# Two-layer hybrid decoder trunk: the opening's first two projections in float32 on h as loaded, with the norm's factor applied afterwards

## The chip, the cores and the metric

The kernel runs on one core of one Trainium2 chip. The metric is the device time of one execution in microseconds (us); the median of three runs is given. Engines are called by their profile names: PE (matrix engine, with PEld its weight loads), DVE (vector), ACT (scalar), POOL (GpSimd) and SP (the queue that issues the loads).

## The reference

A sequence of 528 positions (16 learned meta tokens and 512 real ones) with 1024 features goes through two layers. Everything is float32.

```
def mixer_sublayer(h, pre_g, ...):
    u = rms_norm(h, pre_g)                     # h * rsqrt(mean(h*h) + eps) * pre_g
    z = u @ w_in                               # q, k, v, forget logit, conv value and gate, short conv b, c, x
    y_attn = forgetting_attention(q, k, v, log_sigmoid(f_logit + b_forget))
    a = a_val * sigmoid(a_gate)                # conformer module
    a = silu(layer_norm(causal_depthwise_conv(a, 31 taps) + bias))
    y_conv = a @ a_pw_w
    y_sc = sc_b * causal_depthwise_conv(sc_c * sc_x, 3 taps)
    return h + rms_norm(head_rms_norm(concat[y_attn, y_conv, y_sc]) @ w_out, post_g)

def ffn_sublayer(h, ...):
    z = causal_depthwise_conv(rms_norm(h, pre_g) @ w_up, 3 taps)
    return h + rms_norm((silu(g) * up) @ w_down, post_g)

def reference(x, ...):
    h = concat[meta_tokens, x]
    for l in range(2):
        h = ffn_sublayer(mixer_sublayer(h, ...), ...)
    return h[16:]
```

## The kernel before

Activations lie transposed: features on the 128 partitions in KD = 8 blocks `k`, the 528 positions along the free axis. They are worked in two halves of H = 264 positions; `hf` is 0 or 1. So a projection of 128 output columns for one half is a sum over 8 blocks of 128x128 weights times 128x264 activations.

Weights come in chunks of 512 KB in the order in which they are used. A chunk is loaded into a `raw` tile (a ring of three), ACT rounds it into `whi` (L617) and DVE writes the rest into `wlo` (L621). Activations are split in the same way into `uhi` and `ulo` (ACT L816, DVE L817). `mm3` (L642, the matmul is L648) then makes each product out of three matmuls, hi by hi, hi by lo and lo by hi, so one projection of one half is 24 matmuls of 264 columns.

In the planned parts every engine follows an order written out when the kernel is built. `Flow` (L219) keeps, for each engine and for SP, a list of operations with an estimated duration, a priority (the lowest number goes first) and what they wait for; it plays them against estimated times and writes each out when its turn comes. PE is driven by threads that yield what they wait for. On the chip the order of an engine then stands fixed and only its waits move.

The opening, up to the mixer of layer 0, is planned in L1741 to L1755 and runs as follows.

- `load_h` issues `h`, two blocks at a time, the first half ahead of the second; `plan_w` issues the weight chunks. The per-feature vectors `pv` of both layers are loaded through POOL's queue (L405) and DVE scales the gains into `pg` (L407).
- For each half, `Norms.square` has ACT square `h` (L723) and DVE add the squares up (L732). `Norms.factor` sums over the features with matmuls against the constant `om_d` (L772) and makes the factor of the norm in ACT (L782, L785, L786) and DVE (L787, L793).
- `gained` multiplies `h` by the gain (ACT L802, tile `hg`), and `pre_norm` multiplies by the factor (DVE L814) and splits the result into `uhi` and `ulo`.
- `First` holds the first six projections, numbered 0 to 5: conv gate and value for two blocks of 128 features (0 and 1, 2 and 3), short-conv c (4) and x (5). `first_half` starts them for half 0 as soon as its `uhi` and `ulo` are there. Half 1 of the same six projections is started in `mixer` (`firsts`, L945).
- `gated` (L914) evacuates a gate and a value: exp, ln, exp on ACT (L918 to L920), one product on DVE (L921) into `apad`. When both halves of a block are there, `conv_taps` (L937) puts 31 taps for each block on DVE (L929, L932) at the lowest priority; `conv_tail` (L1488) needs the last of them for its means on PE (L1500).

PSUM has eight banks: two pairs for the ring "mm" (0 and 1, 5 and 6), banks 2 and 3 for "s", banks 4 and 7 for "n".

Of the kernel before, what the change touches and what calls it, by code (L numbers as in the profile page):

```python
# [15 lines left out]
P = 128  # L16
# [33 lines left out]
NP = 6  # L50

# [304 lines left out]
def tile_hybrid_trunk(ctx: ExitStack, tc: tile.TileContext, xT, wflat, pv_d, out):  # L356
# [46 lines left out]
    for l in range(DEPTH):  # L403
        pv = T(const, [P, NPV], F32, f"pv{l}")
        nc.gpsimd.dma_start(pv, pv_d[l])  # L405
        pg = T(const, [P, NGAIN], F32, f"pg{l}")
        nc.vector.tensor_scalar_mul(pg, pv[:, :NGAIN], -0.5)  # L407
        pvs.append((pv, pg))

# [47 lines left out]
    def load_h(pool, src, prio=0):  # L457
# [3 lines left out]
            t[:, k0:k0 + 2, half_sl(hf)], src[:, k0:k0 + 2, half_sl(hf)]), prio=prio + 3 * hf, lat=dma_lat(2 * H))  # L461
# [142 lines left out]
    def plan_block(i, prio):  # L604
# [19 lines left out]
        got = flow.op("sp", dma_us(sz), load, prio=prio, lat=dma_lat(sz), takes=[(raws, slot)])  # L624
        ring = split["pw"][chunks[i][1]] if chunks[i][0] == "a_pw_w" else split["wide" if i in wide else "rot"]
        a = act(act_us(sz), high, got, prio=prio, takes=[(ring, b.slot)])
# [33 lines left out]
    class First:  # L660
# [4 lines left out]
        def __init__(self, rhs, n, at):  # L665
            self.rhs, self.n, self.at = rhs, n, at
            self.ws, self.ps, self.tok = [], {}, {}
            self.slot = {(hf, i): Slot() for hf in range(2) for i in range(max(FIRST.values()))}

# [26 lines left out]
    class Norms:  # L696
# [17 lines left out]
        def square(self, key, k, src, n, *after, prio=1):  # L714
# [14 lines left out]
            else:  # L729
                a = act(us, lambda: squares(lambda: self.c_tile(n)), *after, prio=prio, takes=[(self.c, slot)])  # L730
                if k < KD - 2 * apart:
                    s["at"] = dve(dve_us(2 * n), lambda: nc.vector.tensor_add(s["acc"]["c"], s["acc"]["c"], box["c"]),  # L732
                                  a, s["at"], prio=prio)
# [155 lines left out]
    def mixer(l, ypool, first, close_first, spans):  # L889
# [7 lines left out]

        mp = ms.enter_context(tc.tile_pool(name=f"mp{l}", bufs=1, reuse_waits="tile"))
# [6 lines left out]
        conv, apads, sigs = [], [], []  # L905
        for j in range(2):
            sigs.append(T(mp, [P, L], F32, ("sccx", "cxp")[j]))
            apad = T(mp, [P, L + CK - 1], F32, "apad", 2)
            nc.gpsimd.memset(apad[:, :CK - 1], 0.0)
            apads.append(apad)  # L910
            conv.append(T(mp, [P, L], F32, "cacc", 2))
        gated_at = {}

        def gated(hf, j, tok):  # L914
            c = half_sl(hf)
            sig = sigs[j][:, c]
            us = act_us(H)
            a = a0 = act(us, lambda: nc.scalar.activation(sig, first.ps[hf, 2 * j], AF.Exp, scale=-1.0), tok)  # L918
            b = act(us, lambda: nc.scalar.activation(sig, sig, AF.Ln, bias=c_one), a)
            b = act(us, lambda: nc.scalar.activation(sig, sig, AF.Exp, scale=-1.0), b)  # L920
            gated_at[hf, j] = got = dve(dve_us(H), lambda: nc.vector.tensor_mul(  # L921
                apads[j][:, CK - 1 + H * hf:CK - 1 + H * (hf + 1)], first.ps[hf, 2 * j + 1], sig), b, prio=0)
            for i in range(2):
                first.slot[hf, 2 * j + i].close(a0, got)
# [31 lines left out]
        for j in range(2):  # L956
            gated(0, j, first.tok[0, 2 * j + 1])
# [6 lines left out]
        def sc_c(j):  # L964
            t = sc[j] = T(mp, [P, L], F32, "sccx")

            def use(hf, ps, tok):
# [6 lines left out]
        def sc_x(j):  # L974
            t = sc[j]
            cx = T(mp, [P, L + 2], F32, "cxp")
# [10 lines left out]
            def use(hf, ps, tok):  # L987
# [26 lines left out]
        for i, make in ((4, sc_c), (5, sc_x)):  # L1014
            use = make(0)
            for hf in range(2):
                evacs += use(hf, first.ps[hf, i], first.tok[hf, 5])
# [84 lines left out]
        def sc_norm(j):  # L1102
            sq = T(mp, [P, L + 2], F32, "cxp")[:, :L]
# [849 lines left out]
```

## Time and profile before

| | us |
|---|---|
| three runs | 1317.92, 1320.25, 1321.16 |
| median | 1320.25 |
| the profiled execution | 1320.06 |
| its span on the core | 1318.4 |
| PE busy in the span | 1278.1 |
| DVE busy | 859.1 |
| ACT busy | 626.3 |
| POOL busy | 98.9 |

The profile is of one execution. A row of its timeline gives start, duration, engine, line of the kernel, operation, tile written and tiles read, and in brackets how long the engine had been idle before it and what released it. Matmuls overlap in the pipeline, so their pace is the distance between starts and not the duration of one. Instructions of DVE and ACT overlap by a little as well. A float32 matmul shows as two records.

### The profile page before, as it was taken

How to read it: one execution, taken by the hardware profiler on the slowest of the kernel's cores; microseconds unless marked ns; L12 is line 12 of the kernel's file. 1: busy time of each engine (PE TensorE's matmuls, PEld its weight loads, DVE VectorE, ACT ScalarE, POOL GpSimd, SP SyncE). 2: the span in 40 equal slices, each digit the busy share in tenths (PEclk: the TensorE clock that was granted, in tenths of full speed). 3: DMA queues.
4: the chain of work that ended last, by engine and by line, in shares of the span. 5: the costliest groups of instructions: out<-in, count | busy, mean ns of one | idle time of the engine just before them, and what ended most of it. 6: DMA issues, size and time to landing. Idle time of an engine off the chain costs nothing. (4 is left out here: it accounts for less than half of the span.)

```text
span 1318.4 us, 23824 instructions
## 1 busy us (share of the span) xinstructions
PE 1278.1 (97%) x9758; PEld 1223.3 (93%) x9758; DVE 859.1 (65%) x1450; ACT 626.3 (48%) x1176; POOL 98.9 (8%) x255
## 2 busy tenths in 40 slices
PE   5999999999999999999989999999999999999997
PEld 4989898999999999999989898979999799989997
DVE  6588856488633674576575888666877247646764
ACT  7345568555423432234662555685644233323353
POOL 1313321000000000000003223110000000000000
PEclk9999999999999999999989999999999999999999
DMA  7032120602222222223240322116032222232221
GB/s 247 21 98 75 56 75 33 213 30 85 92 97 81 97 86 91 96 86 106 82 163 17 99 82 65 57 54 214 24 97 85 92 97 95 71 108 97 90 71 65
DMA packets 42700, 118.26 MB, mean 90 GB/s; under 512 B 4848, under 2 KB 15088, under 8 KB 42592
## 3 DMA queue, kind: packets, MB, share of 16 engines
q1 hardware_dynamic: 42496, 116.48, 26.6%
q8 instruction: 77, 1.26, 0.4%
q0 software_dynamic: 96, 0.26, 0.1%
q14 instruction: 31, 0.25, 0.1%
HBM read 108.04 MB, written 4.33 MB: 85 GB/s over the span
## 5 line engine op out<-in xcount | busy, mean ns | idle before, releaser
L648 PE MATMUL psum<-uhi,whi 128*128 128x264 f32 (+1 forms) x1984 | 466.9, 288 | 7.4 <-ACT uhi L816 7.4
L648 PE MATMUL psum<-ulo,whi 128*128 128x264 f32 (+1 forms) x1984 | 461.7, 285 | 0.9 <-DVE ulo L817 0.9
L648 PE MATMUL psum<-uhi,wlo 128*128 128x264 f32 (+1 forms) x1984 | 459.7, 284 | 0.0
L648 PEld LDWEIGHTS psum<-uhi,whi 128*128 128x128 f32 x1984 | 333.4, 189 | 11.6 <-ACT uhi L816 8.6
L648 PEld LDWEIGHTS psum<-ulo,whi 128*128 128x128 f32 x1984 | 334.2, 190 | 1.9 <-DVE ulo L817 1.5
L648 PEld LDWEIGHTS psum<-uhi,wlo 128*128 128x128 f32 x1984 | 334.0, 190 | 0.0
L648 PE MATMUL psum<-yhi,whi 128*128 128x264 f32 (+3 forms) x840 | 235.2, 304 | 1.4 <-ACT yp L1885 1.0
L648 PE MATMUL psum<-ylo,whi 128*128 128x264 f32 (+3 forms) x840 | 232.6, 300 | 1.0 <-DVE ylo L1085 0.8
L648 PE MATMUL psum<-yhi,wlo 128*128 128x264 f32 (+3 forms) x840 | 231.7, 299 | 0.5 <-DVE wlo L621 0.5
L503 ACT CAST whi<-raw 128x1024 fp32r<-128x1024 f32 (+1 forms) x110 | 113.5, 1033 | 212.5 <-PE psum L648 198.9
L504 DVE TENSOR_TENSOR wlo<-raw,whi 128x1024 fp32r<-128x1024 f32 (+1 forms) x110 | 132.0, 1201 | 81.5 <-ACT whi L503 79.5
L648 PEld LDWEIGHTS psum<-yhi,whi 128*128 128x128 f32 x840 | 150.0, 188 | 10.2 <-ACT yp L1885 1.4
L648 PEld LDWEIGHTS psum<-ylo,whi 128*128 128x128 f32 x840 | 150.0, 188 | 7.5 <-DVE ylo L1085 2.0
L648 PEld LDWEIGHTS psum<-yhi,wlo 128*128 128x128 f32 x840 | 150.2, 188 | 6.1 <-DVE wlo L621 0.9
L1834 DVE SCALAR_TENSOR_TENSOR c<-z,pv,c 128x528 f32<-128x528 f32 (+1 forms) x176 | 132.2, 757 | 2.7
L621 DVE TENSOR_TENSOR wlo<-raw,whi 128x1024 fp32r<-128x1024 f32 (+2 forms) x86 | 102.5, 1207 | 43.0 <-ACT whi L617 42.5
L617 ACT CAST whi<-raw 128x1024 fp32r<-128x1024 f32 (+2 forms) x86 | 87.9, 1035 | 35.8 <-DMA raw<-in_w_dram 17.4
L932 DVE SCALAR_TENSOR_TENSOR cacc<-apad,pv,cacc 128x528 f32<-128x528 f32 x120 | 87.6, 773 | 0.5
L1852 ACT CAST yhi<-c 128x528 fp32r<-128x528 f32 (+1 forms) x44 | 27.6, 628 | 111.3 <-DVE c L1848 111.3
L1844 ACT ACTIVATE c<-c 128x528 f32<-128x528 f32 (+1 forms) x44 | 28.2, 640 | 81.7 <-DVE c L1834 81.7
L1832 ACT ACTIVATE c<-z,pv 128x528 f32<-128x528 f32 (+1 forms) x88 | 63.5, 728 | 0.0
L1797 DVE TENSOR_TENSOR z<-psum,rz 128x528 f32<-128x528 f32 x40 | 28.3, 709 | 53.7 <-PE psum L648 52.1
(199 smaller groups left out, 1422.1 us busy)
## 6 DMA issues: line engine op xcount, KB each, us to landing
raw<-in_w_dram SPq DMA_DIRECT2D x160, 512.0 KB
raw<-in_w_dram SPq DMA_DIRECT2D x32, 448.0 KB
h<-in_x_dram SPq DMA_DIRECT2D x16, 264.0 KB
raw<-in_w_dram SPq DMA_DIRECT2D x4, 528.0 KB
q<-q SPq DMA_DIRECT2D x16, 132.0 KB
k<-k SPq DMA_DIRECT2D x16, 132.0 KB
h_dram<-h SPq DMA_DIRECT2D x4, 528.0 KB
h<-h_dram SPq DMA_DIRECT2D x8, 264.0 KB
```

What stands on the lines that cost most here:

```text
L503: nc.scalar.copy(hi[:, :sz], raw[:, :sz])
L504: nc.vector.tensor_sub(lo[:, :sz], raw[:, :sz], hi[:, :sz].bitcast(F32))
L617: nc.scalar.copy(box["hi"][:, :sz], box["raw"][:, :sz])
L621: nc.vector.tensor_sub(lo[:, :sz], box["raw"][:, :sz], box["hi"][:, :sz].bitcast(F32))
L648: nc.tensor.matmul(d, lhsT=w[a][:, k, cols], rhs=rhs(b, k, hf), start=start and i == 0 and p == 0, stop=stop and i == n - 1 and p == 2)
L932: nc.vector.scalar_tensor_tensor(conv[j], in0=src, in1=conv[j], scalar=col("a_dw_w", CK * j + i), op0=ALU.mult, op1=ALU.add)
L1797: nc.vector.tensor_mul(two(t[:, off:]), srcs[0], two(rz))
L1832: nc.scalar.activation(dst, src[:, 2:2 + 2 * fw], AF.Copy, scale=wtap(2, t))
L1834: nc.vector.scalar_tensor_tensor(dst, in0=src[:, i:i + 2 * fw], scalar=wtap(i, t), in1=dst, op0=ALU.mult, op1=ALU.add)
L1844: silu = nc.scalar.activation(cs[0], cs[0], AF.Silu)
L1852: nc.scalar.copy(ghi, cs[0])
```

## The change

- **Two projections on h as loaded.** Projections 0 and 1 of half 0 become 8 float32 matmuls each on `h` itself. Their weights are multiplied by the gain first, projection 0 by DVE, projection 1 by POOL, each in two pieces of 128x512, into tiles that the mixer uses later (`apad`, `cacc`).
- **The factor of the norm afterwards.** Projections 2 to 5 of half 0 use the split of `h` times the gain (`u_raw`: ACT for hi, DVE for lo, held in `ypool`), without the factor. The factor of half 0 (`rz0`) is applied when the six products leave PSUM: in `gated` by two more DVE products, in `sc_c` by two DVE products in place of an ACT copy. Half 0 of `uhi` and `ulo`, which later projections read, is still made, by `normed`, with priority after half 1.
- **Half 1** is as before, but the gain and the factor are applied by one DVE instruction for each block in place of ACT L802 and DVE L814.
- **Sums of squares** of both halves are added by POOL in place of DVE (six additions of 128x528).
- **Loads.** The gains of layer 0 come first on SP, then `h` and the halves of chunks 0 and 1 in turn, chunks 2 and 3, then half 1 of `h` in turn with chunks 4 and 5. Chunks 0 and 1 have tiles of their own beside the ring of three. The rest of the vectors follows on SP, behind these; POOL issues no load.
- **Warm-up.** 24 matmuls of 264 columns on a tile of ones go ahead of everything on PE.
- `ypool` and the tiles of the conv and short conv (`Front`, pool `mq`) are opened ahead of the opening's pool.

```diff
-        nc.gpsimd.dma_start(pv, pv_d[l])
...
-        nc.vector.tensor_scalar_mul(pg, pv[:, :NGAIN], -0.5)
+    nc.sync.dma_start(pvs[0][0][:, :NGAIN], pv_d[0][:, :NGAIN])
+    nc.vector.tensor_scalar_mul(pvs[0][1], pvs[0][0][:, :NGAIN], -0.5)
...
+        def alone(self, hf, both, *ids, whole=None):
+            slots = [(yield from flow.grab(pring[0]["mm" if both else "s"], self.slot[hf, ids[0]]))]
+            t = mmt(slots[0].buf) if both else psum[:, slots[0].buf]
+            for j, i in enumerate(ids):
+                self.ps[hf, i] = t[:, j, :self.n[hf]] if both else t[:, :self.n[hf]]
+                if i < 2:
+                    for k in range(KD):
+                        yield whole[i](k)
+                        nc.tensor.matmul(self.ps[hf, i], lhsT=whole[2][i][k // 4][:, k % 4], rhs=whole[3](k), start=k == 0, stop=k == KD - 1)
+                        self.tok[hf, i] = flow.mm(mm4_us(self.n[hf]))
+                        yield
+                    continue
+                yield [self.ws[i].tok]
+                for k in range(KD):
+                    yield [When(lambda: self.at.get((hf, k)))]
+                    mm3({hf: self.ps[hf, i]}, self.ws[i].w, [k], self.rhs, start=k == 0, stop=k == KD - 1)
...
+                        s["at"] = gp(add, lambda: nc.gpsimd.tensor_add(s["acc"]["c"], s["acc"]["c"], box["c"]),
+                                     a, s["at"], prio=prio)
...
+        def gated(self, hf, j, tok, rz=None, rz_at=None):
...
+            if rz is not None:
+                a = b = dve(dve_us(H), lambda: nc.vector.tensor_mul(sig, gate, rz), tok, rz_at, prio=0)
...
+            if rz is not None:
+                b = dve(dve_us(H), lambda: nc.vector.tensor_mul(sig, sig, rz), b, prio=0)
...
+                if rz is not None:
+                    e = dve(dve_us(H), lambda: nc.vector.tensor_mul(t[:, c], ps, rz), tok, prio=0)
+                    sc_at[j, "c", hf] = dve(dve_us(H), lambda: nc.vector.tensor_mul(t[:, c], t[:, c], rz), e, prio=0)
+                    return [e]
...
+        warm = T(sp, [P, H], F32R, "warm", 1)
+        nc.vector.memset(warm.bitcast(F32), 1.0)
+        for i in range(WARM):
+            nc.tensor.matmul(psum[:, 7, :H], lhsT=warm[:, :P], rhs=warm, start=True, stop=True)
...
+        def with_gain(i, j, raw, got):
+            c = slice(4 * j, 4 * j + 4)
+            eng, on, us = ((nc.vector, dve, dve_us(4 * P)), (nc.gpsimd, gp, 1.2))[i]
+            wg_at[i].append(on(us, lambda: eng.tensor_mul(
+                wg[i][j], raw()[:, 4 * P * j:4 * P * (j + 1)].rearrange("p (k n) -> p k n", n=P),
+                g0[:, c].unsqueeze(2).to_broadcast([P, 4, P])), got, prio=-1))
...
+        plan_block(0, 0.6, loads=[(0.01, 1.5), (0.03, 1.5)], also=lambda *a: with_gain(0, *a))
+        plan_block(1, 0.6, loads=[(0.1, 1.5), (0.11, 1.5)], also=lambda *a: with_gain(1, *a))
+        h, h_at = load_h(sp, xT, apart=0.27, step=0.01, late=1.5)
+        [plan_block(i, 0.2 + 0.02 * i) for i in range(wpos[0], FIRST["ffn_w_down"])]; wpos[0] = FIRST["ffn_w_down"]
+        flow.op("sp", 0.4, lambda: nc.sync.dma_start(pvs[0][0][:, NGAIN:], pv_d[0][:, NGAIN:]), prio=3.5)
+        pv1 = flow.op("sp", 0.4, lambda: nc.sync.dma_start(pvs[1][0], pv_d[1]), prio=3.5, lat=2.0)
...
+        for k in range(KD):
+            hk, hi, lo, gc = h[:, k, :H], u_raw[0][k], u_raw[1][k], g0[:, k:k + 1]
+            c = act(act_us(H) + 0.06, lambda hk=hk, hi=hi, gc=gc: nc.scalar.activation(hi, hk, AF.Copy, scale=gc),
+                    h_at[0, k - k % 2], prio=0)
+            d = dve(stt_us(H), lambda hk=hk, hi=hi, lo=lo, gc=gc: nc.vector.scalar_tensor_tensor(
+                lo, in0=hk, scalar=gc, in1=hi.bitcast(F32), op0=ALU.mult, op1=ALU.subtract), c, prio=0)
...
+                reads.setdefault((hf, k), []).append(
+                    norms.square(("h", hf), k, h[:, k:k + 2, half_sl(hf)], H, h_at[hf, k], prio=0.3 - 0.08 * hf, add=1.2))
...
+        def normed(hf, prio):
...
+            yield from norms.factor(key, H, out=None if hf else rz0)
...
+                f = [dve(stt_us(H), lambda k=k, i=i: nc.vector.scalar_tensor_tensor(
+                    h[:, k + i, c], in0=h[:, k + i, c], scalar=g0[:, k + i:k + i + 1], in1=s["r"],
+                    op0=ALU.mult, op1=ALU.mult), *f, prio=prio + 0.01 * k) for i in range(2)]
+                hi = act(act_us(2 * H), lambda k=k: nc.scalar.copy(uhi[:, k:k + 2, c], h[:, k:k + 2, c]), *f,
+                         prio=prio + 0.01 * k)
+                lo = dve(dve_us(2 * H), lambda k=k: nc.vector.tensor_sub(
+                    ulo[:, k:k + 2, c], h[:, k:k + 2, c], uhi[:, k:k + 2, c].bitcast(F32)), hi, prio=prio + 0.01 * k)
...
+        def opening():
+            for j in range(2):
+                yield from first.alone(0, True, 2 * j, 2 * j + 1, whole=(
+                    lambda k: [wg_at[0][k // 4], h_at[0, k - k % 2]], lambda k: [wg_at[1][k // 4], h_at[0, k - k % 2]],
+                    wg, lambda k: h[:, k, :H]))
+                front.gated(0, j, first.tok[0, 2 * j + 1], rz0, rz_at)
+            for i in (4, 5):
+                yield from first.alone(0, False, i)
...
+        flow.thread(normed(0, 1.2))
+        flow.thread(normed(1, 0.7))
+        flow.thread(opening())
```

More of the change, by code (lines that the diff above doesn't have):

```diff
@@ L50 @@
 NP = 6
+WARM, WARM_US = 24, 4.5
 _COLS = {}
@@ L902, in mixer @@
         zero = Tok(0.0)
[L905 to L924, printed above, removed]
+        conv, apads, gated_at, gated = front.conv, front.apads, front.at, front.gated
         def tap(j, i):
@@ L954, in firsts @@
             yield from first.steps(1, (True, 4, 5))
-        for j in range(2):
-            gated(0, j, first.tok[0, 2 * j + 1])
+        if not begun_front:
+            for j in range(2):
+                gated(0, j, first.tok[0, 2 * j + 1])
         flow.thread(firsts())
@@ new lines, in tile_hybrid_trunk @@
+        rz_at = When(lambda: [norms.sums["h", 0]["r_at"]] if "r_at" in norms.sums["h", 0] else None)
+        def opening():
+            for j in range(2):
+                yield from first.alone(0, True, 2 * j, 2 * j + 1, whole=(
[4 more added lines that the diff above has]
+                yield from first.alone(0, False, i)
```

123 lines of the change are left out of this document (94 added, 29 removed).

## The prediction

> **What bounds the kernel now.** I read the page first, then the busy time by stretches, then PE's waits up to 130 us, then the timeline of the opening, engine by engine. The page and the three stretches (busy us, records in brackets, granted clock, DMA share, GB/s):
>
> ```profile
> span 1318.4 us, 23824 instructions
> PE 1278.1 (97%) x9758; PEld 1223.3 (93%) x9758; DVE 859.1 (65%) x1450; ACT 626.3 (48%) x1176; POOL 98.9 (8%) x255
> 0.00:17.00 17.00, 2.10 (x4) 1.17 (x4) 8.22 (x13) 12.73 (x22) 4.30 (x25) 1.00 0.88 301
> 17.00:38.00 21.00, 20.33 (x144) 19.90 (x145) 17.49 (x24) 14.79 (x26) 0.19 (x2) 1.00 0.44 149
> 38.00:1318.40 1280.40, 1255.66 (x9612) 1202.27 (x9610) 833.35 (x1415) 598.73 (x1129) 94.42 (x228) 1.00 0.26 86
> ```
>
> PE is the bound: idle for 1318.4 - 1278.1 = 40.3 us, 14.9 of them in the first 17 us and 24.7 spread over the last 1280. Only the first part can be attacked by this change. PE's waits there (total, times, longest) and its timeline:
>
> ```profile
> PE psum L772 <- DVE acc L732: 8.7, 1, 8.7
> PE psum L648 <- ACT uhi L816: 6.3, 1, 6.3
> 8.66 2.10 PE L772 MATMUL psum<-acc,om_d 128*128 128x264 f32 x4 [8.66 <-DVE acc L732]
> 17.07 0.59 PE L648 MATMUL psum<-uhi,whi 128*128 128x264 f32 x1 [6.31 <-ACT uhi L816]
> 18.26 0.59 PE L648 MATMUL psum<-ulo,whi 128*128 128x264 f32 x1 [0.60 <-DVE ulo L817]
> 19.31 0.42 PE L648 MATMUL psum<-uhi,wlo 128*128 128x264 f32 x1
> 19.53 0.42 PE L648 MATMUL psum<-uhi,whi 128*128 128x264 f32 x1
> ...
> 22.37 0.28 PE L648 MATMUL psum<-ulo,whi 128*128 128x264 f32 x1
> 22.48 0.28 PE L648 MATMUL psum<-uhi,wlo 128*128 128x264 f32 x1
> ...
> 25.05 0.28 PE L648 MATMUL psum<-uhi,wlo 128*128 128x264 f32 x1
> 25.16 0.29 PE L648 MATMUL psum<-uhi,whi 128*128 128x264 f32 x1
> 28.86 1.05 PE L772 MATMUL psum<-acc,om_d 128*128 128x264 f32 x4
> 29.55 0.48 PE L648 MATMUL psum<-uhi,whi 128*128 128x264 f32 x1
> 29.87 0.28 PE L648 MATMUL psum<-ulo,whi 128*128 128x264 f32 x1
> ```
>
> PE waits for the sum of squares until 8.66 and for the normalised first half until 17.07. It then runs at 0.22 us between starts until about 22.2 and at 0.12 us after that: about 18 matmuls cost 0.1 us more each, 1.8 us. The granted clock is 1.00 in all stretches and does not show this step; the pace does. [...]
>
> Half 0 of the six projections is 6 x 24 = 144 split matmuls. The second stretch holds 144 records, 4 of them L772, so 4 are left at 38.0 and half 1 starts at 38.0 + 4 x 0.12 = 38.4. From there on PE runs on nearly without a break, so the time hangs on S, the start of half 1: profiled time = 1320.06 - (38.4 - S) + whatever the rest loses. The 1320.06 of the profiled execution is 1.66 above its span and within 0.2 of the median 1320.25.
>
> **PE's own sum after the change.** A float32 matmul of 264 columns, from L772 at 28.86 to the regular place of the next matmul: L648 at 29.87 less one step is 29.75, so 0.89 us for two, 0.445 each. Projections 0 and 1: 16 x 0.445 = 7.1. Projections 2 to 5: 96 x 0.1215 (pace at 25 us) = 11.7. Two norm sums: 2 x 0.89 = 1.8. Together 20.6 us. Against three split matmuls (0.365) float32 costs 16 x 0.08 = 1.3 us more; the norm sum of half 0 (0.9) moves from idle time into the stream.
>
> **When PE can begin.** Loads, the engines that follow them, and DVE's group of additions up to 38.2 us (busy us, mean ns of one, idle before):
>
> ```profile
> 0.81 1.97 SPq L460 DMA_DIRECT2D h<-in_x_dram  x4
> 3.55 0.65 ACT L723 ACTIVATE acc<-h 128x528 f32<-128x528 f32 x1 [1.46 <-DMA h<-in_x_dram]
> 6.32 1.33 ACT L723 ACTIVATE c<-h 128x528 f32<-128x528 f32 x2 [0.34 <-DMA h<-in_x_dram]
> GB/s 0 0 0 27 205 287 342 411 333 368 256 382 395 381 393 369 410 418 418 411 353 387 387 378 365 369 227 434 336 98 147 328 328 279 246 270 221 164 16 0
> L732 DVE TENSOR_TENSOR acc<-acc,c 128x528 f32<-128x528 f32 x6 | 4.2, 707 | 1.6 <-ACT c L723 1.3
> ```
>
> The first 0.26 MB of `h` are there at 3.5, the third at 6.3, and the queue moves some 0.39 MB per us (the GB/s row, half-us slices up to 20 us). With the small gains load ahead (+0.5 us): first `h` about 4, first half of chunk 0 near 5, last of the first half of `h` near 8, chunk 1 in halves at 8.5 and 9.2, chunk 2 at 10.5, chunk 3 at 12, chunk 4 at 14, last of half 1 at 16. DVE needs 0.7 us for a piece of gained weights (128x512; L732 takes 0.71 for 528 columns), so projection 0 can start near 6. The warm-up covers that: 24 matmuls x 0.22 = 5.3 us from about 1 us. It costs nothing while it ends before the first gained weights; if its tile of ones is written late, behind the gains on DVE, projection 0 starts 2 us later, which the wait for projection 1's weights half absorbs. Its gain is the 1.8 us of slow pace.
>
> So S is at least 6.2 + 20.6 = 26.8, that is 11.6 us earlier than now.
>
> **What ACT, DVE and POOL must do by then.** Mean ns per instruction, from the other groups up to 38.2 us, L866's group of the whole span and two single rows:
>
> ```profile
> L621 DVE TENSOR_TENSOR wlo<-raw,whi 128x1024 fp32r<-128x1024 f32 (+1 forms) x8 | 9.8, 1231 | 3.6 <-ACT whi L617 3.6
> L817 DVE TENSOR_TENSOR ulo<-hg,uhi 128x528 fp32r<-128x528 f32 x8 | 5.4, 703 | 0.7 <-ACT uhi L816 0.7
> L793 DVE SCALAR_TENSOR_TENSOR rs<-rs 128x264 f32<-128x264 f32 x2 | 0.9, 434 | 0.1
> L617 ACT CAST whi<-raw 128x1024 fp32r<-128x1024 f32 (+1 forms) x8 | 8.4, 1047 | 0.6 <-DMA raw<-in_w_dram 0.6
> L802 ACT ACTIVATE hg<-h,pg 128x264 f32<-128x264 f32 x16 | 6.9, 506 | 0.7 <-DVE pg L407 0.7
> L816 ACT CAST uhi<-hg 128x528 fp32r<-128x528 f32 x8 | 5.0, 635 | 3.8 <-DVE hg L814 3.8
> L723 ACT ACTIVATE c<-h 128x528 f32<-128x528 f32 x6 | 3.7, 638 | 0.4 <-DMA h<-in_x_dram 0.3
> L866 DVE SCALAR_TENSOR_TENSOR ulo<-h,pg,uhi 128x264 fp32r<-128x264 f32 x24 | 11.0, 491 | 0.0
> 33.06 1.87 ACT L816 CAST uhi<-hg 128x528 fp32r<-128x528 f32 x3 [1.71 <-DVE hg L814]
> 40.01 0.43 DVE L921 TENSOR_TENSOR apad<-psum,sccx 128x264 f32<-128x264 f32 x1 [1.86 <-ACT sccx L920]
> ```
>
> ACT up to the first pair of half 1: 8 hi parts x 0.51, 8 squares x 0.64, 6 chunks x 1.05, two norms of three passes and two gates of three passes at 0.43 (as DVE's passes of 264 columns), one pair 0.64: 4.1 + 5.1 + 6.3 + 2.6 + 2.6 + 0.6 = 21.3 us from 4, which ends at 25.3. The removed products by the gain (16 x 0.51) are half replaced by the hi parts. ACT just fits.
>
> DVE: gained weights 2 x 0.7, lo parts 8 x 0.49, six chunks 7.4, two norms 4 x 0.43, two gates 6 x 0.43 (four more than now, 1.7 us), first pair 2 x 0.49 + 0.70: 1.4 + 3.9 + 7.4 + 1.7 + 2.6 + 1.7 = 18.7 us from 5, which ends at 23.7. The half-0 normalisation (8 x 0.49 + 4 x 0.70 = 6.7) is put behind half 1 and lies beside half 1's 17.5 us on PE. The six additions (4.2) are gone from DVE. In `sc_c` one ACT copy becomes two DVE products, 0.9 us, with DVE idle around it. The loads of the remaining vectors wait behind all of these on SP and are wanted only by the taps.
>
> POOL's rows:
>
> ```profile
> L1391 POOL TENSOR_SCALAR_AFFINE_SELECT pf<-pf x64: 289/295/1492, 94.7 to 874.0; 128x128 f32<-128x128 f32 x64
> L1348 POOL TENSOR_SCALAR dm<-ident,mcol x80: 270/374/1286, 86.7 to 846.2; 128x128 fp32r<-128x128 f32 x64, 16x16 fp32r<-16x16 f32 x16
> 89.90 1.22 DVE L621 TENSOR_TENSOR wlo<-raw,whi 128x1024 fp32r<-128x1024 f32 x1
> 90.08 1.28 POOL L1348 TENSOR_SCALAR dm<-ident,mcol 128x128 fp32r<-128x128 f32 x1 [0.99 <-DVE mcol L1340]
> ```
>
> POOL takes six additions and two gained pieces (the groups give min, median and max ns). No POOL row has two tensor inputs, so I bound it: below by DVE's 0.71, above by twice 528/128 of POOL's undisturbed 0.295 for 128 columns and one input (median of L1391), 2.4. I take one pass in proportion, 1.2 us; eight are 9.6 us.
>
> [...]
>
> These rows also speak against the change: POOL's row at 90.08 lies beside a DVE instruction with two inputs from SBUF, and it took 1.28 instead of 0.37 (median), until just after DVE ended at 91.12. So additions on POOL do not simply leave DVE. Suppose POOL and those DVE instructions never overlap: 18.7 less the eight of 0.43 that read PSUM (3.4) is 15.3, plus 9.6 is 24.9 from 5, so the first pair of half 1 is there at 29.9. Without any exclusion it is PE's 26.8. DVE has gaps (it waits for ACT's chunks), so part of POOL's time falls into them. I take S = 29.0, nearer to the excluded end, as DVE is busy 18.7 of 24 us. The later pairs of half 1 cost DVE 1.7 us each against 1.46 for PE (12 x 0.1215), three pairs: 0.7 us more. **Forecast: 1320.06 - (38.4 - 29.0) + 0.7 = 1311.4 us.**
>
> **Rivals.**
>
> *The POOL chain ends last.* PE's order is fixed, and the norm sum of half 0 stands ahead of the later projections. Its chain is additions on POOL, with the gained weights of projection 1 in the same queue: five instructions from about 7.6 us, 13.6 undisturbed. If each is held by one chunk on DVE (1.28 - 0.37 = 0.9), it is 18, and the same again in half 1 puts its factor 4 us later than in the forecast: S = 33.0, time 1314.7 + 0.7 = 1315.4. For it: the row at 90.08. Against: DVE's short instructions early on. [...]
>
> *PE's own work is the only limit.* S = 26.8 and no loss after: 1308.5. For it: ACT and DVE fit by their sums. Against: 25.3 on ACT leaves 1.5 us for every hop and late load.
>
> *The second half is not earlier.* Its `uhi` is made from 33.06 on now, after ACT and DVE work that the change keeps and adds to (hi and lo parts, gates). If all the delays add up, the first pair comes at 36.5: 1320.06 - 1.9 = 1318.2, within 0.3%.
>
> *Slower: DVE's backlog reaches the conv tail.* The last tap and its reader on PE:
>
> ```profile
> 169.58 0.76 DVE L932 SCALAR_TENSOR_TENSOR cacc<-apad,pv,cacc 128x528 f32<-128x528 f32 x1
> 184.17 0.77 DVE L1504 TENSOR_TENSOR cacc<-cacc,psum 128x264 f32<-128x264 f32 x2 [1.10 <-PE psum L1500]
> ```
>
> Taps run at the lowest priority and end at 170.3, 13.8 us ahead of their reader. PE comes 9 us earlier, which leaves 5. DVE's added work is 3.9 + 1.4 + 1.7 + 0.9, and 16 x 0.49 in place of L814's eight (taken at L817's 0.70: 2.2 more), less 4.2: 5.9 us, plus up to 9.6 held by POOL; DVE's idle time up to 38 us (38.0 - 8.2 - 17.5 = 12.3) takes it. It decides only when the backlog passes 12.3 + 5; each us more is a us of PE if the order has nothing else in that place. To lose the whole gain of 8.7 and 5 us it takes 13.7 more than that: 1325.
>
> **How the numbers follow.** Forecast 0.42, POOL chain 0.25, PE alone 0.15, second half not earlier 0.11, slower 0.07. Faster by over 0.3% (4 us, about what a measurement of this kernel can tell from no change) is the first three, 0.82; within 0.3% 0.11; slower 0.07. The range 1307 to 1317 holds the first three and leaves out the last two; its lower end is PE alone less 1.5 us, since the order of the mixer is planned anew and some of PE's 24.7 us of later idle time lies there.
>
> **What would show it.** Right: projection 0 starts near 6 us at a pace of 0.445; split matmuls run at 0.12 from their first; PE has no wait over 3 us after it; half 1 starts at 28 to 30; POOL's additions take 1.0 to 1.5 us, and longer beside DVE's chunks; the mixer's waits stay. Wrong: L772 or projection 1 waits over 3 us for POOL (first rival); the start of half 1 waits for DVE or ACT until 33 or later (third); L1500 waits for a tap (fourth); or the pace of 0.22 comes back because PE went idle between the warm-up and projection 1.

## The result and the profile after

The changed kernel takes 1316.66 us (median of 16 executions, 1312.88 to 1318.85) against 1320.11 us before (16 executions, 1317.43 to 1323.27): a ratio of 0.9971, 95% interval 0.9961 to 0.9982. The forecast was 1311.4, 8.7 us less than before; 3.5 came. The interval leaves out 1, though 3.5 us is under the 4 that the prediction took for measurable, and the time lies inside the stated range. The profiled execution of the changed kernel was its fastest, 1312.88 us at a mean granted clock of 0.998; the 16 together have 0.9944, and 58 executions of the kernel before, timed beside the runs below, have 0.997. That difference turns out to be a part of the answer.

The page of the kernel after, and the same three stretches as before (busy us with records, clock, DMA share, GB/s):

```profile
span 1311.2 us, 23868 instructions
PE 1281.2 (98%) x9766; PEld 1225.1 (93%) x9766; DVE 869.9 (66%) x1469; ACT 622.2 (47%) x1167; POOL 108.3 (8%) x261
0.00:17.00 17.00, 13.32 (x59) 11.40 (x59) 11.41 (x14) 11.05 (x18) 9.65 (x30) 1.00 0.87 295
17.00:38.00 21.00, 19.83 (x150) 18.96 (x151) 20.79 (x36) 14.59 (x27) 4.78 (x3) 1.00 0.30 105
38.00:1311.20 1273.20, 1248.07 (x9560) 1194.72 (x9558) 837.73 (x1421) 596.54 (x1124) 93.90 (x228) 1.00 0.28 87
```

In the first 17 us PE works 13.3 us (5.4 of them the warm-up) instead of 2.1. DVE is busy 20.8 of the next 21 us, where it was 17.5. PE's waits up to 60 us (total, times, longest):

```profile
PE psum L667 <- DVE wlo L624: 1.9, 1, 1.9
PE psum L667 <- ACT uhi L1870: 0.8, 1, 0.8
PE psum L698 <- POOL cacc L1829: 0.4, 1, 0.4
PE psum L667 <- DVE ulo L1872: 0.4, 1, 0.4
```

and the timeline of the opening after, PE first, then DVE and POOL, then the forget gate of layer 0 (start, duration, idle before):

```profile
1.26 5.37 PE L1819 MATMUL psum<-warm 128*128 128x264 f32 x24 [1.26 <-DVE warm L1817]
6.47 4.08 PE L698 MATMUL psum<-h,apad 128*128 128x264 f32 x16
10.97 3.83 PE L698 MATMUL psum<-h,cacc 128*128 128x264 f32 x16 [0.43 <-POOL cacc L1829]
16.91 0.39 PE L667 MATMUL psum<-yhi,wlo 128*128 128x264 f32 x1 [1.88 <-DVE wlo L624]
17.14 1.05 PE L815 MATMUL psum<-acc,om_d 128*128 128x264 f32 x4
31.45 0.39 PE L667 MATMUL psum<-uhi,whi 128*128 128x264 f32 x1 [0.79 <-ACT uhi L1870]
32.22 0.39 PE L667 MATMUL psum<-ulo,whi 128*128 128x264 f32 x1 [0.38 <-DVE ulo L1872]
...
8.33 7.40 DVE L1848 SCALAR_TENSOR_TENSOR ylo<-h,pg,yhi 128x264 fp32r<-128x264 f32 x6
22.45 1.43 DVE L1866 SCALAR_TENSOR_TENSOR h<-h,pg,rz 128x264 f32<-128x264 f32 x2
8.36 1.31 POOL L775 TENSOR_TENSOR acc<-acc,c 128x528 f32<-128x528 f32 x1 [4.41 <-ACT c L762]
9.88 2.23 POOL L1829 TENSOR_TENSOR cacc<-raw,pg 128x512 f32<-128x512 f32 x2 [0.20 <-DMA raw<-in_w_dram]
...
72.58 0.41 PE L1283 MATMUL psum<-fpre,ones_r 128*128 128x40 f32 x2 [0.71 <-DVE fpre L1278]
74.50 0.60 PE L1292 MATMUL psum<-ident,gt 128*8 128x128 f32 x4 [0.71 <-DVE gt L1284]
```

PE begins at 6.47, as forecast. Half 1 runs without a break from 32.22, where one of its matmuls is done, so S, the effective start of half 1, is 32.1: 6.3 us earlier than 38.4. The span is 7.2 shorter.

### The profile page after: what moved, and what is told of

It reads as the page before. It is cut to its first block, busy times and chain, and to the rows that moved or that the text cites. A ratio compares the mean times of both kernels' runs of the same rounds, so it can differ in the third digit from the quotient of the medians.

```text
span 1311.2 us, 23868 instructions
## 1 busy us (share of the span) xinstructions
PE 1281.2 (98%) x9766; PEld 1225.1 (93%) x9766; DVE 869.9 (66%) x1469; ACT 622.2 (47%) x1167; POOL 108.3 (8%) x261
## 5 line engine op out<-in xcount | busy, mean ns | idle before, releaser
L667 PE MATMUL psum<-uhi,whi 128*128 128x264 f32 (+1 forms) x1936 | 451.4, 287 | 1.9 <-ACT uhi L859 1.1
L667 PE MATMUL psum<-ulo,whi 128*128 128x264 f32 (+1 forms) x1936 | 446.6, 284 | 0.7 <-DVE ulo L1872 0.4
L667 PE MATMUL psum<-uhi,wlo 128*128 128x264 f32 (+1 forms) x1936 | 444.7, 283 | 0.0
L667 PEld LDWEIGHTS psum<-uhi,whi 128*128 128x128 f32 x1936 | 322.7, 189 | 5.5 <-issue 2.4
L667 PEld LDWEIGHTS psum<-ulo,whi 128*128 128x128 f32 x1936 | 323.7, 189 | 1.6 <-DVE ulo L860 0.7
L667 PEld LDWEIGHTS psum<-uhi,wlo 128*128 128x128 f32 x1936 | 323.6, 189 | 0.0
L667 PE MATMUL psum<-yhi,whi 128*128 128x264 f32 (+3 forms) x872 | 245.2, 304 | 1.5 <-ACT yp L2025 1.0
L667 PE MATMUL psum<-yhi,wlo 128*128 128x264 f32 (+3 forms) x872 | 240.9, 299 | 2.4 <-DVE wlo L624 2.4
L667 PE MATMUL psum<-ylo,whi 128*128 128x264 f32 (+3 forms) x872 | 241.2, 299 | 1.0 <-DVE ylo L1152 0.8
L667 PEld LDWEIGHTS psum<-ylo,whi 128*128 128x128 f32 x872 | 156.2, 188 | 7.6 <-DVE ylo L1152 2.0
```

The lines of the kernel that those rows point to most:

```text
L667: nc.tensor.matmul(d, lhsT=w[a][:, k, cols], rhs=rhs(b, k, hf), start=start and i == 0 and p == 0, stop=stop and i == n - 1 and p == 2)
```

## Experiments

The theories named in the expectations are "POOL holds DVE" (six additions and two gained pieces on POOL slow the DVE instructions beside them down, and half 1 is late by that) and "clock" (more of its executions run some stretches at half clock). All runs were timed in five rounds beside the kernel before, unless said otherwise.

**The same kernel again.** No edit.

> The changed kernel once more, to see how its executions differ. In the profiled execution (1312.88 us, granted clock 0.998) half 1 starts at about 32.1 us instead of 38.4, which is worth 6.3 us; the median of 16 executions is only 3.5 us under the one of before, and its granted clock is mostly 0.992 to 0.996. Theory (clock): in most executions the clock falls to half in the opening, in PE's wait of 1.9 us for a chunk's low part at 14.8 us or at the half-1 start at 30.5 us; then the recorded clock steps show a stretch of some 3.4 to 6.8 us at half clock before 40 us, and times rise by about 1 us for each 0.1% of clock. Rival (later loss): the stretches at half clock all lie at the layer boundary near 660 us and at the end, as in the profiled execution, and there is no step in the opening; then the gain that is missing was never there and the profiled execution was only lucky.

1315.01 us (7 executions, mean clock 0.9951), ratio 0.9967 (0.9954 to 0.9981). Again the profiled execution was the fastest (1312.6 at 0.998) and shows no stretch at half clock before 661 us, so it could not show the step that the theory wanted. The 7 executions here and the 16 above differ by 1.65 us in their medians; together with the single one below, all 24 have 1316.66 us.

**The additions back on DVE.**

```
-  norms.square(("h", hf), k, ..., prio=0.3 - 0.08 * hf, add=1.2))
+  norms.square(("h", hf), k, ..., prio=0.3 - 0.08 * hf))
```

> The changed kernel with the six additions of squares back on DVE; the gained weights of projection 1 stay on POOL. Theory (POOL holds DVE): in the profile after, six low parts on DVE took 7.4 us from 8.33 on, 1.2 us each instead of 0.49, while POOL's two-input work of 1.1 to 1.6 us each ran; on DVE the six additions cost 4.2 us. So DVE is free some 2 us earlier, the wait of 1.9 us at 14.8 us shrinks under 1 us, half 1 starts at 29 to 30 us and the time falls by 2 to 3 us against the changed kernel (ratio to before about 0.995); with the clock theory by up to 3 us more. Rival (DVE is full either way): the additions take the place of the stalls, half 1 starts at 32 us and the time is within 1 us of the changed kernel.

1316.28 us (clock 0.9944), ratio 0.9968 (0.9957 to 0.9979). The opening of its timeline, DVE and PE:

```profile
8.37 3.29 DVE L1848 SCALAR_TENSOR_TENSOR ylo<-h,pg,yhi 128x264 fp32r<-128x264 f32 x6
30.58 2.42 DVE L624 TENSOR_TENSOR wlo<-raw,whi 128x1056 fp32r<-128x1056 f32 x2
32.92 0.70 DVE L1872 TENSOR_TENSOR ulo<-h,uhi 128x528 fp32r<-128x528 f32 x1
28.56 0.28 PE L667 MATMUL psum<-uhi,whi 128*128 128x264 f32 x1
33.68 0.43 PE L667 MATMUL psum<-ulo,whi 128*128 128x264 f32 x1 [2.72 <-DVE ulo L1872]
```

The same six low parts take 3.29 us instead of 7.40: POOL did hold DVE, for 4.1 us in this group alone. PE reaches half 1 at 28.56. But the planner now puts the low parts of two later chunks (30.58) ahead of the second pair, and PE waits 2.72 us for it; the clock is then at half from 33.89 to 37.30. So the hold is shown, and that taking it away pays by itself is not: what stood behind it in DVE's order came next. Neither expectation fits: half 1 starts as early as the theory had it, and the time is what the rival had.

**Nothing on POOL.** As above, and the gained weights of projection 1 on DVE too.

```
-  ((nc.vector, dve, dve_us(4 * P)), (nc.gpsimd, gp, 1.2))[i]
+  ((nc.vector, dve, dve_us(4 * P)), (nc.vector, dve, dve_us(4 * P)))[i]
```

> As adds_dve, and the gained weights of projection 1 on DVE too: POOL has no work in the opening after its constants. Theory (POOL holds DVE): two pieces of 1.1 us on POOL, each of which can hold DVE, become 1.4 us on DVE; half 1 starts as in adds_dve or up to 1 us earlier. Rival (DVE is full either way): 1.4 us later than adds_dve.

1319.55 us (11 executions, clock 0.9925), ratio 0.9992 (0.9983 to 1.0002): the gain is gone.

```profile
32.22 0.59 PE L667 MATMUL psum<-uhi,whi 128*128 128x264 f32 x1 [4.01 <-ACT uhi L1870]
```

PE stands at half 1's first pair for 4.0 us, and the matmuls behind it start 0.22 us apart until 37.1 and 0.12 from 37.3 on. The time is 3.3 us more than with the pieces on POOL, where the rival had 1.4. DVE is full with or without POOL, and here the low parts of two later chunks (23.87 and 29.10) stood ahead of that pair; so the order before half 1's pairs matters as much as the amount.

**No warm-up.** `WARM, WARM_US = 0, 4.5`, so that the plan stays as it is.

> The changed kernel without the 24 warm-up matmuls, the planned order unchanged. Projection 0 then starts near 6.3 us at half pace, 0.89 us for a float32 matmul, until about 10 us: it ends 1.8 to 2 us later and projection 1 too. PE then waits 1.9 us for a chunk's low part at 14.8 us, so theory (POOL holds DVE) has most of it hidden there: 0 to 1 us slower than the changed kernel. Rival (the warm-up is the gain): 2 us or more slower, half 1 at 34 us.

1316.41 us (clock 0.9948), ratio 0.997 (0.9958 to 0.9981), the changed kernel's time.

```profile
5.87 6.74 PE L698 MATMUL psum<-h,apad 128*128 128x264 f32 x16 [5.87 <-DVE apad L1829]
16.58 0.39 PE L667 MATMUL psum<-yhi,wlo 128*128 128x264 f32 x1 [0.17 <-DVE wlo L624]
```

Projection 0 takes 6.74 us without the warm-up instead of 4.08 with it, and the wait for `wlo` shrinks from 1.88 to 0.17: the slower start is hidden behind a wait. A gain from the warm-up is not seen here.

**PE's waits of the opening filled.** 16 matmuls whose result nobody reads ahead of projection 2, 10 ahead of half 1.

```
+  if i == 2:
+      dummies(self.ps[hf, i], 16)
...
+  if items[0] == 0:      # the first steps of half 1
+      dummies(self.ps[hf, 0], 10)
```

> The changed kernel with 26 more matmuls on TensorE whose result nobody reads: 16 ahead of projection 2 of half 0, where PE waits 1.9 us for the low part of its chunk (15.0 to 16.9 us), and 10 ahead of half 1's first matmul, where it waits 0.8 and 0.4 us (30.7 to 32.2). At 0.11 to 0.12 us each they fill 1.8 and 1.2 us of idle time, and no other engine's order changes. Theory 'clock': part of the expected gain is lost because a wait of PE in the opening makes the granted clock fall to one half for one or two stretches of 3.4 us in part of the executions. With the gaps filled, the mean granted clock over the executions rises from 0.9945 to about 0.997 and the median falls by 2 to 3 us, to about 1314 (ratio to the kernel before near 0.9955). Rival 'lost elsewhere': the clock is lost later in the kernel (at the layer boundary), whatever the opening does; then the clock stays near 0.9945 and the median at 1315 to 1317 (0.997).

1316.73 us (clock 0.9942), ratio 0.997 (0.9959 to 0.9982). The waits of 1.9 and 0.8 us are gone and the clock is as low as it was (0.9942 against 0.9944): it is not lost in the opening. The theory had the wrong place, and the rival was right.

**The changed kernel, one profiled execution.** No edit.

> The changed kernel once more, one profiled execution. Theory 'clock': if this execution is one of the slower ones (1316 us or more), its granted clock shows one or two stretches of 3.4 us at one half before 40 us, which the first profile (1312.9 us) does not have; if it is a fast one it shows none there. Rival 'lost elsewhere': a slow execution has the stretches at the layer boundary or later only.

1318.33 us at 0.992. Its clock is 0.50 in stretches of 3.41 us that start at 74.72, 204.43, 661.81 (two) and 859.78, none before 40 us. Two of them, each with the stretch before it (length, busy us with records of PE, PEld, DVE, ACT and POOL, then the granted clock, DMA share and GB/s):

```profile
71.31:74.72 3.41, 1.98 (x16) 1.39 (x14) 3.19 (x10) 0.91 (x2) 0.00 (x0) 1.00 0.85 279
74.72:78.13 3.41, 3.41 (x17) 3.38 (x17) 2.69 (x6) 1.33 (x4) 0.00 (x0) 0.50 0.65 197
201.01:204.43 3.42, 2.15 (x15) 1.69 (x14) 2.64 (x6) 1.40 (x6) 2.08 (x4) 1.00 0.52 186
204.43:207.84 3.41, 3.41 (x16) 3.19 (x15) 0.00 (x0) 2.58 (x8) 0.08 (x1) 0.50 0.16 61
```

The same places in the first profile of the changed kernel, on its own grid of 3.41 us:

```profile
71.00:74.41 3.41, 2.08 (x17) 1.75 (x15) 3.17 (x11) 1.49 (x3) 0.00 (x0) 1.00 0.90 320
74.41:77.82 3.41, 3.32 (x27) 3.03 (x28) 3.41 (x7) 1.39 (x4) 0.00 (x0) 1.00 0.56 147
658.09:661.50 3.41, 1.31 (x5) 0.83 (x5) 3.41 (x7) 3.15 (x7) 0.00 (x0) 1.00 0.47 184
661.50:664.91 3.41, 3.04 (x13) 2.75 (x14) 3.38 (x8) 3.41 (x8) 0.00 (x0) 0.50 0.00 0
```

Of the three stretches in these rows in which PE idled 1.3 to 1.4 us, two were followed by one at half clock (busy 1.98 and 2.15) and one was not (2.08); the one with 2.1 idle (busy 1.31) was. In the one execution both waits of the forget gate fall into one stretch, and 17 matmuls follow in 3.41 us where the other has 27; in the other the second wait ends 0.09 us after its stretch. This execution has four stretches at half more than the first and is 5.45 us longer, 1.4 us for each.

**The rest of the work held back.** The additions are on DVE, as in adds_dve, and besides, the normalisation of half 0 and the chunks from the seventh on wait until half 1's last pair is made. So three things differ from the changed kernel.

```
+  u1 = When(lambda first=first: first.at.get((1, KD - 2)))
-  plan_w(after_mixer[0])
+  plan_w(after_mixer[0], hold=[u1])          # act(..., *got, *hold)
-  f = [s["r_at"], *reads[hf, k]]
+  f = [s["r_at"], *reads[hf, k]] + ([] if hf else [u1])
```

> The six additions are on DVE, and everything that half 1's first pairs do not need (the normalisation of half 0 and the chunks from the seventh on, on ACT and DVE) waits until half 1's last pair is made. Theory 'POOL holds DVE, and the order of the rest costs the remainder': with the additions on DVE the six low parts take 3.3 us, and the 2.7 us wait of PE for the second pair (behind two chunks of 1.2 us on DVE) goes: half 1 starts at about 29.0, with a wait of 0.7 us for the second pair, so effectively 29.7 against 32.1 in the changed kernel: 2.4 us less at the same clock, a median of 1313 to 1314.5 (ratio 0.9952). Rival 'DVE is full either way': what is put off comes back as a wait at the end of half 1 or in the mixer (for the normalised half 0 or for a chunk at 45 to 60 us), and the median stays at 1316 (0.997).

1312.45 us (5 executions, clock 0.9960), ratio 0.9943 (0.993 to 0.9955).

```profile
28.70 0.28 PE L667 MATMUL psum<-uhi,whi 128*128 128x264 f32 x1
29.23 0.39 PE L667 MATMUL psum<-ulo,whi 128*128 128x264 f32 x1 [0.24 <-DVE ulo L1873]
31.46 0.39 PE L667 MATMUL psum<-ulo,whi 128*128 128x264 f32 x1 [0.37 <-DVE ulo L1873]
```

Half 1 starts at 28.7 and waits 0.6 us in all. At the end of the six projections it is 2.2 us ahead of the changed kernel's first profile (last matmul 47.40 against 49.62), at the layer boundary 1.2 (639.16 against 640.33); a wait of 0.5 us for a norm sum at 252.69 is new. So of 2.2 us about half was still there at the layer boundary; at full clock, below, the difference from the changed kernel is 2.9 us.

**The float32 part alone undone.** Projections 0 and 1 of half 0 are split on the parts of `h` like the others; no gained weights. Chunks 0 and 1, which PE now needs first, also get the highest priority on ACT and DVE, so a little more than the float32 part differs.

```
-  yield from first.alone(0, True, 2 * j, 2 * j + 1, whole=(...))
+  yield from first.alone(0, True, 2 * j, 2 * j + 1)
...
-  plan_block(0, 0.6, ...)
+  plan_block(0, -1, ...)
-  plan_block(1, 0.6, ...)
+  plan_block(1, -0.5, ...)
```

> The changed kernel without the float32 projections: projections 0 and 1 of half 0 are split like the others, on the high and low parts of h times the norm weight, and no gained weights are made on DVE and POOL (their tiles stay unused). Everything else of the change is kept. If the float32 part is what lets PE begin early and what pays (the forecast's step 'projection 0 can start near 6'), PE now waits for chunk 0's two parts and for the low part of h until 9 to 10 us, and since 144 split matmuls and two norm sums take 19.3 us, half 1 starts at 30 or later and the time is that of the changed kernel or 1 us more (1316 to 1318). Rival 'the second half is set by DVE and POOL': PE has slack ahead of half 1, so the later start costs nothing, two fewer pieces on POOL and two on DVE (0.7 us each) bring half 1's first pair forward, and half 1 starts at 29.5 to 31: 1 to 2 us less (1314.5 to 1316).

1315.22 us (5 executions, clock 0.9940), ratio 0.9955 (0.9941 to 0.9968). PE's waits up to 60 us:

```profile
PE psum L815 <- POOL acc L775: 2.2, 2, 1.6
PE psum L667 <- ACT whi L620: 1.9, 1, 1.9
```

PE's first split matmul is at 8.7, PE waits 2.2 us for POOL's chain, the split matmuls of half 0 take 297 to 310 ns on average where those of half 1 take 284 to 286, and half 1 begins at 33.5 in this profile, 2 us later than in the changed kernel; yet the time is 1.4 us less, with overlapping intervals. Neither expectation fits both numbers. That the float32 projections, the first item of the change, gain anything is not shown.

**The waits of the mixers filled.** In the kernel before, in the changed one and in late_rest, matmuls without a reader ahead of those that wait longest:

```
+  dummies(ps[:, :H], 6)            # forget gate, ahead of each of its two waits
+  if hd == 6 and qa and b in (0, 2):
+      dummies(psum[:, free_bank, :H], 8 if b == 0 else 11)
+  dummies(ps, 19)                  # layer boundary, norm sum of h
+  dummies(self.ps[0, 0], 8)        # layer boundary, first uhi
```

> The kernel before, with matmuls whose result nobody reads put ahead of those matmuls of the mixers and of the layer boundary for which PE waits longest: per layer 6 + 6 at the forget gate (waits of 0.7 to 1.1 us), 8 + 11 in the seventh head of attention (0.9 and 1.26), and 19 + 8 once, at the layer boundary (2.2 and 1.1). Each is meant to fit into the wait (0.11 us apiece); the opening and the order of the other engines are untouched. Theory 'clock by windows': the granted clock is decided in stretches of 3.41 us; a stretch in which PE idles for more than about 1.3 us makes the next one run at half, and whether two waits fall into one stretch depends on where the grid of stretches lies, which differs between executions. With the waits filled the mean clock rises from 0.9968 to about 0.999 and the median falls by 2.5 to 3.5 us, to about 1317 (ratio 0.9977). Rival 'the clock is not set by these waits': clock and time stay (0.9968, 1320) or the time rises by the filling.

1320.39 us (11 executions, clock 0.9984), ratio 0.9999 (0.999 to 1.0009).

> The changed kernel with the same filling. Theory 'clock by windows': part of the gain was lost since more of its executions have two waits of the mixers in one stretch of 3.41 us (mean clock 0.9945 against 0.9968), not by anything slower in its work. Filled, its clock is that of the filled kernel before, about 0.999, its median falls by 5 us to 1311 to 1312 (ratio to the kernel before 0.9935), and it lies 5.5 to 7 us under the filled kernel before, which is the gain at equal clocks. Rival 'the work after the opening is slower': clock and time stay near 0.9945 and 1316, or both filled kernels fall by the same 3 us and their difference stays at 3.5.

1314.09 us (clock 0.9984), ratio 0.9954 (0.994 to 0.9968).

> late_rest (additions on DVE, the rest of the work held back until half 1 is made) with the same filling: the candidate for the best version. late_rest measured 1312.45 at a mean clock of 0.996, with half 1 done 2.2 us earlier than in the changed kernel, of which 0.9 was lost again by the layer boundary. Theory 'clock by windows': at a clock of 0.999 the median is 1309 to 1310.5 (ratio 0.992). Rival 'the two gains are the same gain' (late_rest was only lucky with the grid): the median is that of after_fill, 1311 to 1312.

1311.42 us (clock 0.9982), ratio 0.9932 (0.9919 to 0.9945).

The clock rises in all three to the same 0.998, and at equal clocks the change is worth 1320.39 - 1314.09 = 6.3 us. The times of the last two fell less than expected, and that of the kernel before did not fall at all, as the 19 matmuls stood in the wrong place, here in the filled kernel before:

```profile
657.70 2.47 PE L663 MATMUL psum<-yhi 128*128 128x264 f32 x19
667.99 1.24 PE L782 MATMUL psum<-acc,om_d 128*128 128x264 f32 x3 [2.23 <-DVE acc L740]
```

PE's next matmul began at 660.01, so they cost 2.3 us, and the wait of 2.23 stayed.

**The same, mended:** 18 matmuls ahead of the sum that waits.

```
-  norms.fill["h", 0] = 19, rhs(0, ks[-1], 0)
+  norms.fill["y", 1] = 18, rhs(0, ks[-1], 0)
```

> before_fill with one thing mended: its 19 matmuls for the layer boundary ran at 657.7 to 659.9 us, where PE had no wait, and cost 2.2 us by themselves, while the 2.2 us wait stayed. Now 18 stand directly ahead of the matmul that waits. Theory 'clock by windows': no stretch at half is left between the opening and the end; mean clock 0.999 or more, median about 1317 (before_fill's 1320.4 less 2.2 and less the last stretch's 1.2). Rival 'filling buys nothing': 1318.5 or more.

1317.22 us (8 executions, 1316.42 to 1317.73, clock 0.9990), ratio 0.9972 (0.9961 to 0.9982).

> The changed kernel with the same mended filling. Theory 'clock by windows': clock 0.999, median 1311 to 1312, and 6.3 us under before_fill2 (after_fill lay 6.3 under before_fill at the same mean clock 0.9984), which is the 38.4 to 32.1 us by which half 1 starts earlier. Rival 'the work after the opening gives part of it back': the difference is 4 us or less once no time is lost to the clock in either.

1311.33 us (5 executions, 1310.92 to 1311.73, clock 0.9992), ratio 0.9928 (0.9915 to 0.9941). The forget gate and the layer boundary now, in the stretches of the unfilled profile:

```profile
71.00:74.41 3.41, 3.41 (x29) 3.11 (x28) 3.17 (x11) 1.28 (x2) 0.00 (x0) 1.00 0.88 303
658.09:661.50 3.41, 3.17 (x19) 2.43 (x17) 3.41 (x7) 3.16 (x7) 0.00 (x0) 1.00 0.32 125
661.50:664.91 3.41, 3.01 (x24) 3.01 (x25) 3.37 (x7) 3.41 (x7) 0.00 (x0) 1.00 0.00 0
```

Both places now stand at full clock, the profiled execution has a mean clock of 1.000 (a stretch of 3.41 us at half would take 0.0013 from it), and the executions lie within 1.3 us of each other. DVE's busy time in these stretches is that of the unfilled profile above (3.17, 3.41, 3.38).

> late_rest with the mended filling, the candidate for the best version. late_mixfill measured 1311.42 with 2.1 us of matmuls in no wait. Theory: 1309 to 1309.8, 8.5 to 9 us under before_fill2 less what the layer boundary takes back (up to 0.9): that would be the forecast's gain of 8.7, reached with the additions on DVE and the rest of the work held back. Rival 'the two gains are one': it equals after_fill2 within 1 us.

1308.44 us (5 executions, 1308.20 to 1309.30, clock 0.9996), ratio 0.9908 (0.9893 to 0.9923). This is the best version, below both kernels and 8.8 us below the filled kernel before.

## Why the prediction was wrong

Of the 8.7 us that the sum gave against the profiled 1320.06, 3.45 came (1320.11 - 1316.66). The missing 5.2 divide into three.

**S was 32.1 and not 29.0 with 0.7 of later waits: 2.4 us.** The step that failed is DVE's sum. Its groups after, up to 38 us, and POOL's (busy us, mean ns of one, idle before), then four rows of DVE's timeline:

```profile
L1848 DVE SCALAR_TENSOR_TENSOR ylo<-h,pg,yhi 128x264 fp32r<-128x264 f32 x8 | 8.4, 1095 | 1.8 <-ACT yhi L1846 1.8
L624 DVE TENSOR_TENSOR wlo<-raw,whi 128x1024 fp32r<-128x1024 f32 x6 | 8.2, 1398 | 0.0
L836 DVE SCALAR_TENSOR_TENSOR rz<-rs 128x264 f32<-128x264 f32 x1 | 1.3, 1269 | 0.0
L775 POOL TENSOR_TENSOR acc<-acc,c 128x528 f32<-128x528 f32 x6 | 9.2, 1527 | 7.7 <-ACT c L762 7.6
L1829 POOL TENSOR_TENSOR cacc<-raw,pg 128x512 f32<-128x512 f32 x2 | 2.2, 1134 | 0.2 <-DMA raw<-in_w_dram 0.2
7.72 0.69 DVE L1829 TENSOR_TENSOR apad<-raw,pg 128x512 f32<-128x512 f32 x1 [1.50 <-DMA raw<-in_w_dram]
20.73 1.27 DVE L836 SCALAR_TENSOR_TENSOR rz<-rs 128x264 f32<-128x264 f32 x1
30.25 1.29 DVE L1866 SCALAR_TENSOR_TENSOR h<-h,pg,rs 128x264 f32<-128x264 f32 x3
31.46 0.70 DVE L1872 TENSOR_TENSOR ulo<-h,uhi 128x528 fp32r<-128x528 f32 x1
```

The eight low parts were costed at 0.49 us each and took 1.10 on average (8.4 instead of 3.9), the six chunks 8.2 instead of 7.4, one factor step 1.27 instead of 0.43: 6.1 us more on DVE. In return POOL took 4.2 us of additions off DVE and kept 1.4 us of gained pieces (as measured on DVE in no_pool) away from it. With the pieces alone on POOL (adds_dve) the eight low parts take 4.3 us, so most of the hold came from the additions.

The rows that the prediction had show the hold from POOL's side alone. It allowed for it on DVE by an exclusion, but sized that too small. It let 0.9 of POOL's 9.6 us fall into gaps of DVE (29.0 instead of 29.9), and from 7.72 to the first pair of half 1 DVE had none. It left out eight of the ten instructions of 0.43 us as readers of PSUM; by the code six are. The other four are the products on the gate (L960) and the factor's last step (L836), and one of these took 1.27 us at 20.73 beside POOL. With six left out its bound would have been 30.7. And POOL took 11.4 us by its rows, not 9.6, though the 1.3 to 2.0 us of its additions, all of one shape, suggest that some of this is time in which it was itself held. That DVE was slowed by POOL is seen in the 7.40 against 3.29 us for the same six instructions, with the additions on POOL and without; by what mechanism was not shown. Two of DVE's readers of PSUM beside POOL's additions (20.36 to 23.19) were not longer: 0.42 us at 20.28 and 0.43 at 22.10.

Second, the order. The prediction put the half-0 normalisation behind half 1; the plan ran two pieces of it at 22.45 (1.43 us) ahead, and two products of half 1's second pair at 30.25 (some 0.8 us) ahead of the first pair's `ulo`.

How much each did can be estimated from these rows. The prediction's list for DVE ended at 23.7, and its S of 29.0 left 5.3 us for the hold. The first `ulo` was done at 32.2, 8.5 us behind the list's end: 6.1 of hold, 2.2 of order and 1.5 of waiting for a load (at 7.72), less 1.3 in which rows overlap or were shorter than listed. So of the 3.1 us in S the hold beyond its allowance is about 0.8, and order and load are the larger part.

late_rest, which takes the additions off POOL and holds back the later work, has half 1 at 28.7 with 0.6 us of waits, and that is the forecast's S. The later work held back with the additions left on POOL was not run, so the two parts are not separated by a run.

**The clock took 2.4 us more than before.** The prediction has no such term. It let PE's later waits stay as they were, and by their length they nearly did. Filling them gave the kernel before 1320.11 - 1317.22 = 2.9 us and the changed one 1316.66 - 1311.33 = 5.3. One reason is in the timeline after: at 72.58 PE waits 0.71 us for the forget gate's sum, which it did not before, since PE had come forward by 6.0 us at this place (L1282 begins at 71.56, its like before at 77.59) and DVE by 5.2 (`fe` at 70.62, before 75.81). With the old 0.71 us that follows at 74.50 it makes a pair within one stretch of 3.41 us. The rest is where the waits lie on the grid of stretches, which differs between executions; how much of the 2.4 us is this new wait and how much the other shifted pairs was not taken apart. The figure itself is loose: the 7 executions of the same kernel again would give 1.2 us in its place (1315.01 - 1311.33 against 1319.68 - 1317.22).

**The rest, 0.4 us,** lies between the gain in S (6.3) and the difference at full clock (5.9); with executions that differ by 1.3 us it was not followed up.

Point by point:
- PE from 6.47 to half 1: it began as forecast. Projection 0 took 4.1 us against 3.6, the second float32 one was at the forecast pace; waits of 3.5 us (0.4, 1.9, 0.8 and 0.4) make up the distance from 26.8 for the most part.
- Warm-up: hidden, as forecast, but its gain of 1.8 us was not seen (no_warm).
- ACT was never last by itself: its `uhi`, which let PE go on at 31.45, followed DVE's product.
- POOL's additions: 1.3 to 2.0 us each against the estimate of 1.2, which is under every one of them. The forecast's "longer beside DVE's chunks" held: the longest, 2.03 at 17.15, lay beside DVE's chunks (4.62 us from 15.65 on).
- "POOL chain ends last" has the nearest time, 1315.4, by luck and not by its cause: L815 was at 17.14 without a wait of its own, and S was 32.1 by DVE's order. "PE alone" and "second half not earlier" did not happen; of the conv tail's rival nothing was seen.
- "The mixer's waits stay" was right in their sum and missed what they do to the clock.

## What to carry to other kernels

Before work is moved to POOL, count what it does to the DVE instructions that run beside it; here eight instructions, worth 5.6 us on DVE, cost it 6.1. When an opening is shortened by a better order, check in the plan what the busiest engine does ahead of the new critical step; holding back later chunks and a normalisation, with the additions back on DVE, brought 2.9 us at full clock (1311.33 to 1308.44), while the additions alone on DVE brought nothing (1316.28). And compare two kernels by their clock too: a gain of 5.9 us looked like 3.5 because short waits had moved, and 88 matmuls without a reader, placed in waits, gave 5.3 us to the changed kernel.

## What the runs showed of the hardware

- In look the stretches at half clock start at 74.72, 204.43, 661.81 and 859.78, which is 38, 134 and 58 times 3.413 us from one to the next. Where this grid of stretches lies differed between three executions of the changed kernel: at the layer boundary the clock fell to half at 661.26 (again), 661.50 (the first profile) and 661.81 (look).
- The stretch ahead of one at half was not idle throughout: PE was busy for 1.31 of its 3.41 us at 658.09 in the first profile and for 2.15 at 201.01 in look, and two waits of 0.7 us were in the one at 71.31 (look). The 1.3 us of idle time in the expectation of before_fill is not a sharp edge. In the profiles of before (from 22.3 us on, where its pace had risen), after, again and look, each taken on its own grid, seven stretches at full clock with PE busy for 1.31 us or less were followed by one at half; so were three with 1.98, 2.13 and 2.15 (all in look), while 1.90 (again), 1.94 (after) and 2.02 (look), among others, were followed by full clock. None with more than 2.15 was followed by one at half.
- A stretch at half cost 1.4 us of time (5.45 us for four, between the first profile and the one with four more), not the 1.7 that half of 3.41 would be; where the difference went was not taken apart.
